# The first microseconds of an MLP kernel: PSUM copies and casts given to ScalarE, and four differences made in halves

## The chip, the cores and the metric

The kernel runs on one core of one Trainium2 chip. The time is that of one execution on the device, in microseconds (us); lower is better. A time here is the median of several executions, and the range is given where it matters.

The engines are called as the profile calls them: PE is TensorE (PEld its weight loads), DVE is VectorE, ACT is ScalarE, POOL is GpSimd, and SP is SyncE, which issues most DMA transfers. PSUM is the memory that the matmuls here write to; SBUF holds the other tiles of the kernel.

## The reference

```python
x:  8 x 1024 x 1024 f32;  w1: 1024 x 4096 f32;  w2: 4096 x 1024 f32
h = x @ w1
h = 0.5 * h * (1 + np.tanh(np.sqrt(2 / np.pi) * (h + 0.044715 * h ** 3)))
return (h @ w2).astype(np.float32)
```

## The kernel before

The kernel works in f16 on blocks of 1024 tokens. Each of the two matrix products is cut into 2 x 2 blocks and done with seven block products in place of eight. For that it needs differences of blocks of x and sums or differences of blocks of the weights; VectorE makes them. In the table, `A_TERMS` gives for each product the two blocks of x that are subtracted, and `B_TERMS` the blocks of weights.

```python
B_TERMS = {1: ("11", SUB, "22"), 2: ("11", None, None), 3: ("12", ADD, "22"), 4: ("21", ADD, "11"),
           5: ("22", None, None), 6: ("11", ADD, "12"), 7: ("21", ADD, "22")}
A_TERMS = {1: ("11", "22"), 2: ("21", "22"), 3: ("11", None), 4: ("22", None),
           5: ("12", "11"), 6: ("21", "11"), 7: ("12", "22")}
```

Products 3 and 4 use a block of x as it is; products 2 and 5 use a block of the weights as it is. For each chunk of 128 columns of a half of w1 the source has the products in the order 4, 5, 1, 2, 3, 7, 6, with 4 matmuls each; product 6 of a chunk stands behind product 5 of the next.

The first 1024 tokens are brought in by the core itself. Eight tiles of 128 tokens are loaded as f32, transposed on TensorE into PSUM, and copied from PSUM to SBUF as f16. The copies are shared by two engines:

```python
def x_first():
    ...
    for a in (1, 0):                       # tokens 512..1023 first, then 0..511
        for q in range(NQ):                # NQ = 4 tiles of 128 tokens
            load_in_order(flat(xn), x2[r0:r0 + P, :])
            for k in (1, 0):
                ps = psum()
                ...                        # 4 transposes by matmul with the identity
                eng = nc.vector.tensor_copy if k == 0 else nc.scalar.copy
                eng(out=blocks[f"{a + 1}{k + 1}"][:, :, q * P:(q + 1) * P], in_=...)
        if a:
            xs.make(2)                     # difference for product 2
    return xs
```

The weights of the first product come in quads of four chunks. The first quad is loaded column by column, so that work can start after one column. Each column is two loads, one for each half of w1, and each load is cast to f16 in two pieces:

```python
def load_cols(self, c, n):                 # n columns of 128, from column c
    ...
    for b in range(2):                     # the two halves of w1
        cast = (nc.scalar.copy, pool_copy)[b]
        for k in range(2 * KH - kn, -1, -kn):
            load_in_order(st, w1v[b, :, k:k + kn, cs])
            for a in range(k // KH, (k + kn) // KH):
                cast(out=self.raw[f"{a + 1}{b + 1}"][:, :, cs], in_=...)
```

After that the differences of x and the sums of the first columns are made in the order of the products:

```python
if sb == 0:
    quads.append(MadeQuad(0, True, False))
    xs.make(5)
    cs = quads[0].load_cols(0, 1)
    quads[0].sum(4, cs)
    for m in (1, 3, 7, 6):
        if m != 3:
            xs.make(m)
        quads[0].sum(m, cs)
    for c, n in ((1, 1), (2, 2)):
        cs = quads[0].load_cols(c, n)
        for m in SUMS:
            quads[0].sum(m, cs)
```

The instructions of an engine run in one order, which a scheduler fixes when the kernel is built; it need not be the order of the source.

## Time and profile before

| | before |
|---|---|
| median of 3 executions (range) | 1582.91 us (1581.23 to 1582.93) |
| span of the profiled execution | 1577.2 us |
| TensorE busy | 98% of the span |
| first matmul of the first product | 17.69 us |
| start of the second product | 122.34 us |

These are the lines of part 1 of the profile page of the kernel before: busy time of each engine, share of the span and number of instructions.

```profile
PE 1547.1 (98%) x7808; PEld 767.1 (49%) x7808; DVE 1028.8 (65%) x1291; ACT 467.9 (30%) x784; POOL 202.8 (13%) x290
```

TensorE is the limit, and only what lets it start earlier or pause less can help. The next view is the timeline of TensorE in the kernel before, with start and length in us; then engine, line, operation, names, shapes and count, and in brackets the idle time before the group and who ended it.

```profile
17.69 1.04 PE L285 MATMUL ps<-u 128*128 128x512 f16 x4 [2.45 <-DVE u L112]
19.85 8.82 PE L285 MATMUL ps<-u 128*128 128x512 f16 x27 [1.12 <-POOL u L123]
29.37 4.26 PE L285 MATMUL ps<-u 128*128 128x512 f16 x19 [0.70 <-DVE tmp L112]
34.11 2.32 PE L285 MATMUL ps<-u 128*128 128x512 f16 x10 [0.48 <-DVE tmp L112]
...
119.25 1.02 PE L285 MATMUL ps<-u 128*128 128x512 f16 x4 [0.17 <-DVE tmp L112]
120.44 2.06 PE L285 MATMUL ps<-u 128*128 128x512 f16 x8 [0.17 <-DVE tmp L112]
```

Product 4 of the first chunk starts at 17.69 us. Its four matmuls end, and product 5 waits 1.12 us for GpSimd's casts. Two pauses behind VectorE and one behind ScalarE (0.41 us, at 36.84) follow.

Who works in these stretches is told by the timeline of the other engines in the kernel before (VectorE, ScalarE, GpSimd):

```profile
15.28 0.69 DVE L250 CAST u<-ps 128x512 f16<-128x512 f32 x1 [0.64 <-PE ps L241]
16.07 2.70 DVE L112 TENSOR_TENSOR u<-u 128x2048 f16<-128x2048 f16 x3
15.87 1.14 ACT L185 CAST u<-gc 128x512 f16<-128x512 f32 x2 [0.44 <-DMA gc<-in_w_dram]
33.72 1.04 ACT L147 CAST u<-gc 128x1024 f16<-128x1024 f32 x1 [4.37 <-DMA gc<-in_w_dram]
17.71 2.08 POOL L123 CAST u<-gc 128x512 f16<-128x512 f32 x2 [16.41 <-DMA gc<-in_w_dram]
```

VectorE copies the last block until 15.97 us and then goes straight into differences of x. GpSimd needs 2.08 us for two casts, where ScalarE needs 1.14 us for two of the same size. ScalarE stands idle for 4.37 us in front of a cast of the next quad (L147), because its column hasn't landed.

The chain of waits of the kernel before, followed back from the matmuls at 45 us, has these pieces among others (start, length, what):

```profile
17.71 2.09 POOL u L123 x2
...
27.68 6.01 DMA gc<-in_w_dram
...
33.72 1.04 ACT u L147
34.77 2.03 ACT g L295 x4
```

### The profile page before, as it was taken

What the parts mean: (1) busy time and instruction counts of PE and PEld (TensorE: products, weight loads), DVE (VectorE), ACT (ScalarE), POOL (GpSimd) and SP (SyncE); (2) the same over time, 40 slices, a digit from 0 to 9 for tenths busy, and PEclk for the clock granted to TensorE, in tenths of its full rate; (3) what the DMA queues carried; (4) which work ended last, traced back from release to release, by engine and by line L of the source; (5) the groups of instructions that cost most, each with busy time, mean ns of one, the idle gap of its engine ahead of it and who ended that gap; (6) DMA issues with size and microseconds to landing.
All of it is one profiled execution on the core that took longest, in us unless ns stands there. A gap on an engine that the chain in (4) does not pass through costs nothing.

```text
span 1577.2 us, 20360 instructions
## 1 busy us (share of the span) xinstructions
PE 1547.1 (98%) x7808; PEld 767.1 (49%) x7808; DVE 1028.8 (65%) x1291; ACT 467.9 (30%) x784; POOL 202.8 (13%) x290
## 2 busy tenths in 40 slices
PE   7999999999899999999999999999999999999998
PEld 4444444444344455444554445544554445544454
DVE  6875967678775567555665647656575556655564
ACT  4645024410144111441124410344004430044210
POOL 2241010033310012000120001200121001200000
PEclk9999999999999999999999999999999999999999
DMA  9999852399965567735696446954569445663164
GB/s 303 340 327 340 246 205 97 122 302 327 399 184 144 200 252 271 233 107 191 247 314 200 157 153 246 358 151 179 179 239 355 135 186 192 243 234 134 54 233 167
DMA packets 165634, 352.64 MB, mean 224 GB/s; under 512 B 72736, under 2 KB 78880, under 8 KB 164640
## 3 DMA queue, kind: packets, MB, share of 16 engines
q1 hardware_dynamic: 146944, 278.97, 51.1%
q0 software_dynamic: 18592, 72.37, 13.9%
q8 instruction: 61, 1.00, 0.3%
q14 instruction: 37, 0.30, 0.1%
HBM read 272.63 MB, written 93.32 MB: 232 GB/s over the span
## 4 chain that ended last, share of the span: by engine, by line
PE 86%; DMA 8%; DVE 3%; issue 1%; ACT 1%; POOL 0%; SPq 0%; DVEq 0%; ACTq 0%; POOLq 0%
PE ps L285 47%; PE ps L567 33%; PE ps L523 6%; DMA u<-w_d 2%; DVE u L112 2%; DMA u<-raw_d 2%; DMA gc<-in_w_dram 1%; DVE tmp L112 1%; DMA out_dram<-tmp 1%; DMA in_d<-u 1%; DVE gc L112 1%; DMA w_d<-u 1%; DMA xb<-in_x_dram 0%; DMA u<-in_x_dram 0%; DMA u<-in_d 0%
## 5 line engine op out<-in xcount | busy, mean ns | idle before, releaser
L285 PE MATMUL ps<-u 128*128 128x512 f16 x3584 | 782.1, 380 | 10.5 <-ACT tmp L349 4.5
L112 DVE TENSOR_TENSOR tmp<-tmp,ps 128x512 f32<-128x512 f32 x580 | 395.8, 685 | 301.4 <-ACT tmp L349 113.7
L285 PEld LDWEIGHTS <-u 128*128 128x128 f16 x3584 | 351.5, 98 | 438.6 <-issue 17.2
L567 PE MATMUL ps<-u,gc 128*128 128x512 f16 x1792 | 389.7, 379 | 3.9 <-DVE gc L112 3.6
L567 PEld LDWEIGHTS <-gc 128*128 128x128 f16 x1792 | 175.2, 98 | 216.0 <-DVE gc L112 4.6
L295 ACT ACTIVATE g<-tmp 128x512 f16<-128x512 f32 x256 | 161.0, 630 | 287.4 <-DVE tmp L112 287.4
L567 PE MATMUL ps<-u,g 128*128 128x512 f16 x1024 | 223.6, 379 | 0.0
L112 DVE TENSOR_TENSOR u<-u 128x2048 f16<-128x2048 f16 (+2 forms) x170 | 183.4, 1112 | 20.9 <-DMA u<-raw_d 12.3
L295 ACT ACTIVATE g<-ps 128x512 f16<-128x512 f32 x256 | 151.8, 596 | 98.4 <-PE ps L285 97.8
L567 PEld LDWEIGHTS <-g 128*128 128x128 f16 x1024 | 100.2, 98 | 119.6
L112 DVE TENSOR_TENSOR gc<-g,g 128x2048 f16<-128x2048 f16 x112 | 132.9, 1220 | 15.8 <-PE ps L567 15.8
L112 DVE TENSOR_TENSOR u<-u,ps 128x512 f32<-128x512 f32 x144 | 95.7, 681 | 68.7 <-ACT tmp L624 37.3
L381 POOL DMA_DIRECT2D out_dram<-tmp x72 | 39.5, 548 | 778.4 <-ACT tmp L617 593.1
L523 PE MATMUL ps<-u,gc 128*128 128x256 f16 x960 | 109.8, 273 | 0.7
L349 ACT COPY tmp<-ps 128x512 f32<-128x512 f32 x128 | 73.0, 570 | 95.5 <-PE ps L285 95.5
L523 PEld LDWEIGHTS <-gc 128*128 128x128 f16 x960 | 93.8, 98 | 12.8 <-issue 1.8
L112 DVE TENSOR_TENSOR gc<-u 128x2048 f16<-128x2048 f16 x60 | 73.2, 1219 | 39.3 <-PE ps L567 39.3
L112 DVE TENSOR_TENSOR tmp<-ps,tmp 128x512 f32<-128x512 f32 x128 | 88.2, 689 | 5.9 <-PE ps L285 1.1
L112 DVE TENSOR_TENSOR u<-tmp,ps 128x512 f32<-128x512 f32 x24 | 16.5, 687 | 74.8 <-PE ps L567 65.1
L112 DVE TENSOR_TENSOR u<-g,g 128x2048 f16<-128x2048 f16 x48 | 59.4, 1277 | 0.0
L617 ACT COPY tmp<-ps 128x512 f32<-128x512 f32 x24 | 14.1, 586 | 152.0 <-PE ps L567 152.0
L624 ACT COPY tmp<-ps 128x512 f32<-128x512 f32 x24 | 14.0, 585 | 133.5 <-PE ps L567 132.8
(32 smaller groups left out, 351.0 us busy)
## 6 DMA issues: line engine op xcount, KB each, us to landing
u<-w_d SPq DMA_DIRECT2D x172, 512.0 KB, 7.8
u<-raw_d SPq DMA_DIRECT2D x136, 512.0 KB, 7.1
u<-in_d SPq DMA_DIRECT2D x84, 512.0 KB, 6.8
gc<-in_w_dram SPq DMA_DIRECT2D x48, 512.0 KB, 6.5
w_d<-u POOLq DMA_DIRECT2D x40, 512.0 KB, 7.3
out_dram<-tmp POOLq DMA_DIRECT2D x72, 256.0 KB, 3.8
raw_d<-u SPq DMA_DIRECT2D x32, 512.0 KB, 10.0
xb<-in_x_dram POOLq DMA_DIRECT2D x56, 256.0 KB, 11.0
```

The lines of the kernel that those rows point to most:

```text
L112: nc.vector.tensor_tensor(out=out, in0=in0, in1=in1, op=op)
L285: nc.tensor.matmul(bank, lhsT=ops[m][:, k, cs], rhs=xs[m][:, k, :], start=(first and k == 0), stop=(k == KH - 1), skip_group_check=not first,)
L295: gelu_last[0] = nc.scalar.activation(out=g[b][:, c, :], in_=src, func=GELU)
L349: nc.scalar.copy(out=v, in_=pb)
L381: return queue.dma_start(out=out2[r0:r0 + P, o0:o0 + OH], in_=src)
L523: nc.tensor.matmul(bank[:, i * HO:(i + 1) * HO], lhsT=t[:, c, i * P:(i + 1) * P], rhs=y[j][:, c, :], start=(first and i == 0 and c == 0), ...
L567: nc.tensor.matmul(banks[q], lhsT=a, rhs=pieces[c // QC][:, c % QC, :], start=(first and c == 0), stop=(c == NI - 1), skip_group_check=not ...
L617: nc.scalar.copy(out=c21, in_=ps)
L624: nc.scalar.copy(out=c12, in_=ps)
```

## The change

The intent is to shorten the way to the first products. Three things change. (1) The second half of the first column is cast by ScalarE and no longer by GpSimd. (2) The four differences 5, 1, 7 and 6 are made in two halves of 256 tokens: the first halves as soon as two of the last four token tiles have been copied, the second halves where the whole ones stood. (3) All the PSUM copies of the first tokens go to ScalarE, which takes eight of them from VectorE.

```diff
-                cast = (nc.scalar.copy, pool_copy)[b]
+                cast = pool_copy if b and c else nc.scalar.copy
...
-        def make(self, *ms):
+        def make(self, *ms, cols=slice(None)):
             for m in ms:
                 u, v = A_TERMS[m]
-                self[m] = unit(KH, HT)
-                tt(self[m], self.blocks[u], self.blocks[v], SUB)
+                if m not in self:
+                    self[m] = unit(KH, HT)
+                tt(self[m][:, :, cols], self.blocks[u][:, :, cols], self.blocks[v][:, :, cols], SUB)
...
-                    eng = nc.vector.tensor_copy if k == 0 else nc.scalar.copy
-                    eng(
+                    nc.scalar.copy(
                         out=blocks[f"{a + 1}{k + 1}"][:, :, q * P:(q + 1) * P],
                         in_=ps.rearrange("p (j t) -> p j t", t=P),
                     )
+                if a == 0 and q == 1:
+                    xs.make(5, 1, 7, 6, cols=slice(0, HT // 2))
...
-            xs.make(5)
+            rest = slice(HT // 2, HT)
+            xs.make(5, cols=rest)
...
-                    xs.make(m)
+                    xs.make(m, cols=rest)
```

## The prediction

> **What bounds the kernel now.** TensorE. The page has PE busy 98% of 1577.2 us, and the idle time before its matmul groups adds up to only about 22 us. The change touches the start alone: by the instruction order of the two built kernels, PE, ACT, DVE and POOL work the same list of jobs after the first blocks, and the DMA queue's order does not change at all. So all that can be won lies before 37 us, after which PE runs 27 us without a pause (timeline).
>
> **What the start costs now** (timeline, waits, granted clock):
> - x tiles land about 1.29 us apart until 14.04 us; transposes end at 15.24.
> - First real matmuls at 17.69 us, released by DVE: the first w1 column lands at 15.85, ACT casts it until 17.01, but DVE is in a 1.22 us difference (m=5) until 17.29 and only then makes the sum.
> - PE then waits 1.12 us for POOL, whose two casts of the second column take 2.08 us (ACT: 1.14 us).
> - Pauses of 0.70, 0.48 and 0.41 us follow at 29.4, 34.1, 36.8, behind DVE (busy nearly without a break from 20 to 36 us) and behind ACT, which sits 4.37 us in front of a cast whose column has not landed, with gelus queued behind.
> - The granted clock is 0.5 from 18.77 to 25.60 us, about 2.9 us lost from 19.85 on. That is twice the 3.413 us window of the Trainium skill ("TensorE: Matmul & The Clock Gate", The HAM clock gate), so the trace agrees; its phase runs freely.
>
> **What the change moves.**
> - Eight PSUM copies of 0.69 us go from DVE to ACT (0.585 us): ACT then does two per x tile, 1.19 us in 1.29 us. It just keeps up.
> - Four differences (1.22 us each) become eight halves, estimated at 0.65 us; four of them run before the last tokens. About 2.6 us of DVE work leaves the crowded stretch after 16 us.
> - The second column's casts take 1.14 us on ACT instead of 2.08 on POOL: product 5 can start at about 18.9 instead of 19.85.
> - Against it: the last PSUM copy stands on ACT between the two casts of the first column, so it waits for the landing at 15.85; the second halves of 5 and 1 and the first sum then end at about 18.7. I expect the FIRST matmul about 1 us LATER (18.7 us), then no pause before product 5.
> - The cast of the third load comes before a gelu on ACT, so the first load of the next quad is issued about 3 us earlier (now 26.74), and ACT's 4.37 us stall mostly goes.
>
> **Sum.** Pauses of 2.7 us fall to about 1; 1 us is lost at the first matmul; the half clock ends one window earlier or at the same time (0 to 1.7 us). Net gain 0.5 to 2.5 us, expected 1.4 us. Later waits (3.02 us at 173.9, 4.52 at 431) hang on loads that PE's progress releases, so I expect the gain to be kept.
>
> **Time:** 1581.3 us, 8 in 10 between 1579.0 and 1583.2; the three runs of before spread over 1.7 us. Faster by over 2%: 0.01; within 2%: 0.98; slower: 0.01.
>
> **What would show it.** First matmul after 17.69; gap before product 5 near zero; DVE's m=5, 1, 7, 6 halves starting near 12 us; ACT's first 128x1024 cast of the next quad with little wait; PE continuous, about 1 to 2 us ahead at 40 us.
>
> **What would make it wrong.** ACT falling behind the transposes; the clock gate's phase, at the start or at the 4.52 us wait, hiding or doubling the gain; the DMA-filled stretch 137 to 166 us giving the gain back at 173.9.

## The result, and the profile after

| | before | after |
|---|---|---|
| median of 4 executions (range) | 1582.92 us (1581.23 to 1583.69) | 1579.90 us (1578.62 to 1584.12) |
| ratio, 95% interval | | 0.9987 (0.9967 to 1.0007) |
| span of the profiled execution | 1577.2 us | 1576.9 us |
| first matmul of the first product | 17.69 us | 18.59 us |
| start of the second product | 122.34 us | 118.95 us |

A ratio is the mean time of one kernel's fast runs over that of the other's of the same rounds, so it isn't quite the ratio of the medians that are quoted. The kernel after was run again later in five executions beside eleven of the kernel before, with medians of 1576.61 and 1582.44 us and a ratio of 0.9972 (0.9947 to 0.9998). So there is a small gain, some 0.1 to 0.3%, which a single set of rounds could hardly tell from nothing.

The same views of the kernel after. First part 1 of its page:

```profile
PE 1547.7 (98%) x7808; PEld 768.5 (49%) x7808; DVE 1022.3 (65%) x1287; ACT 474.7 (30%) x794; POOL 197.6 (13%) x288
```

VectorE has lost 6.5 us of work and ScalarE has gained 6.8; TensorE is as busy as it was. Its timeline:

```profile
18.59 14.23 PE L287 MATMUL ps<-u 128*128 128x512 f16 x53 [3.44 <-DVE u L112]
33.70 85.41 PE L287 MATMUL ps<-u 128*128 128x512 f16 x395 [0.88 <-DVE tmp L112]
118.95 4.26 PE L570 MATMUL ps<-u,g 128*128 128x512 f16 x19
```

TensorE starts 0.90 us later, but then pauses just once before the second product, for 0.88 us at 33.70. The pause before product 5 is gone, and so are all the small pauses to the end. The second product starts 3.39 us earlier.

The timeline of the other engines in the kernel after (VectorE, ScalarE, GpSimd):

```profile
13.60 3.10 DVE L112 TENSOR_TENSOR u<-u 128x1024 f16<-128x1024 f16 x5 [0.73 <-ACT u L250]
16.91 4.08 DVE L112 TENSOR_TENSOR u<-u 128x1024 f16<-128x1024 f16 x9 [0.21 <-ACT u L250]
15.77 0.62 ACT L185 CAST u<-gc 128x512 f16<-128x512 f32 x1 [0.44 <-DMA gc<-in_w_dram]
16.30 0.58 ACT L250 CAST u<-ps 128x512 f16<-128x512 f32 x1
16.77 0.62 ACT L185 CAST u<-gc 128x512 f16<-128x512 f32 x1
32.27 1.04 ACT L147 CAST u<-gc 128x1024 f16<-128x1024 f32 x1
21.21 1.17 POOL L123 CAST u<-gc 128x512 f16<-128x512 f32 x2 [19.90 <-DMA gc<-in_w_dram]
```

The last copy from PSUM (L250) stands on ScalarE between the two casts of the first column, so it waits for that column to land. This is why the first matmul comes later. The first halves of the differences run before 16.7 us, in time that VectorE had spent on copies or had been waiting. ScalarE no longer waits in front of the next quad's cast (L147). GpSimd's first pair of casts is now that of a later column and takes 1.17 us.

The busy time of the engines from 20 to 34 us (columns: stretch, its length; busy time and instructions of PE, PEld, DVE, ACT, POOL; granted clock; DMA share; GB/s), for the kernel before:

```profile
20.00:34.00 14.00, 12.93 (x46) 5.04 (x45) 12.93 (x22) 4.94 (x9) 4.87 (x5) 0.80 0.90 285
```

And for the kernel after:

```profile
20.00:34.00 14.00, 13.12 (x53) 5.47 (x52) 11.08 (x20) 8.21 (x14) 5.34 (x6) 0.86 0.97 332
```

VectorE is busy for 11.08 us there in place of 12.93, and TensorE fits in 53 matmuls for 46 (a few records can be missing); its granted clock is also higher in this stretch, 0.86 for 0.80. Busy time is work done, and not work that waits: it is one sign only, and below it doesn't tell the better kernels from the others.

**An account of the start.** From the starts of single matmuls in the trace one can say where the time up to the second product goes. The matmuls need 0.216 us each at full clock, some 96.7 us in all; the rest is the start of the first matmul, the pauses, and the time lost at half clock. A pause is counted here from start to start, so a pause that the timeline shows as x costs about x + 0.16 us. The parts add up to the last column within 0.2 us.

| kernel | first matmul | pauses before 40 us | lost at half clock | pauses after 40 us | second product starts |
|---|---|---|---|---|---|
| before | 17.69 | 3.66 | 2.53 | 1.78 | 122.34 |
| after | 18.59 | 1.16 | 2.50 | 0 | 118.95 |
| after, second time | 18.40 | 1.21 | 2.50 | 0 | 118.89 |

The gain of 3.39 us is thus −0.90 for the later start, +2.50 for pauses at the start, +0.03 for the clock and +1.78 for pauses after 40 us.

**Where the lead goes.** In the first pair of traces the lead of 3.39 us ended as 0.3 us. After 122 us both kernels have the same waits: near 170 us, near 430 us and near 1516 us. These vary from execution to execution of the same kernel, and so do the windows of half clock that may follow them. The profile of the kernel after has such windows at 17.1 to 23.9, 170.7 to 174.1 and 426.7 to 433.5 us; that of before at 18.8 to 25.6 and 431.8 to 435.2 us only. In the second trace of the kernel after, those at 16.8 and 170.4 us were the only ones, and its span was 1573.2 us. The four to eleven executions of one kernel in the same rounds spread over 2.5 to 23 us. This is why the start of the second product is used below to compare kernels: it stands ahead of all those waits. In the two traces of the kernel after it repeated to 0.06 us; but the last kernel of this document, whose instructions come in the same order until 163 us, has it at 119.34 us (first matmul 18.86). So one program's mark varies by some 0.45 us in three traces, and a smaller difference between kernels says nothing. The whole time is given too.

### The profile page after: what moved, and what is told of

Read it like the earlier page. It is cut to its first block, busy times and chain, and to the rows that moved or that the text cites. A ratio compares the mean times of both kernels' runs of the same rounds, so it can differ in the third digit from the quotient of the medians.

```text
span 1576.9 us, 20366 instructions
## 1 busy us (share of the span) xinstructions
PE 1547.7 (98%) x7808; PEld 768.5 (49%) x7808; DVE 1022.3 (65%) x1287; ACT 474.7 (30%) x794; POOL 197.6 (13%) x288
## 4 chain that ended last, share of the span: by engine, by line
PE 89%; DMA 6%; DVE 3%; issue 1%; SPq 0%; ACT 0%; DVEq 0%; ACTq 0%
PE ps L287 48%; PE ps L570 35%; PE ps L526 6%; DMA raw_d<-u 2%; DVE u L112 2%; DMA u<-raw_d 2%; DMA u<-w_d 1%; DVE tmp L112 1%; DMA gc<-in_w_dram 1%; DVE gc L112 1%; SPq L120 0%; DMA u<-in_d 0%; ACT tmp L352 0%; ACT u L185 0%; DVE tmp L446 0%
## 5 line engine op out<-in xcount | busy, mean ns | idle before, releaser
L112 DVE TENSOR_TENSOR u<-tmp,ps 128x512 f32<-128x512 f32 x24 | 16.5, 688 | 74.8 <-PE ps L570 65.1
```

Of the source, the lines that this page charges most:

```text
L112: nc.vector.tensor_tensor(out=out, in0=in0, in1=in1, op=op)
```

## The experiments

### The three parts, one at a time and two at a time

The theory at this point: either one of the three parts carries the gain alone, or they need each other. The rival to all three was that ScalarE's stall of 4.37 us, which the chain of waits shows, is what was removed, by whichever part.

**Part 1 alone: the casts.**

```diff
-                cast = (nc.scalar.copy, pool_copy)[b]
+                cast = pool_copy if b and c else nc.scalar.copy
```

> Before, with only the casts of the first columns all on ScalarE. Work-moved theory (each part helps by the work it takes off the crowded engine): first real matmul stays at 17.7 us, the 1.12 us pause before product 5 falls under 0.3, and the first matmul of the second product (before: 122.34 us, after: 118.95) comes 0.8 to 1.5 us earlier. Order theory (the gain is that the halved differences make the build place ScalarE's first cast of the next quad behind four gelus): the pause before product 5 goes, but ScalarE still stands about 4 us before that cast, the pauses near 34 and 37 us stay, and the second product starts at most 0.7 us earlier.

Measured: 1582.08 us beside 1581.00, ratio 1.0013 (0.9977 to 1.0049). First matmul 17.92, second product 122.22 us. The pause before product 5 is gone, but the pauses before 40 us still add up to 3.45 us: what was saved at 19 us is waited for at 24.0 and 33.5.

**Part 3 alone: the copies.**

```diff
-                    eng = nc.vector.tensor_copy if k == 0 else nc.scalar.copy
-                    eng(
+                    nc.scalar.copy(
```

> Before, with only all PSUM copies of the first x blocks on ScalarE. Both theories: ScalarE keeps up with the transposes, first matmul at 17.7 us (the whole difference of 1.22 us still stands before the first sum), pause before product 5 stays near 1.1 us, second product starts within 0.5 us of before's 122.34. Work-moved theory allows up to 0.5 us gain, order theory none.

Measured: 1582.83 us, ratio 1.0014 (0.9991 to 1.0038). First matmul 17.70, second product 123.17 us. There's no gain; the pauses only move, 3.23 us before 40 us and 3.02 after.

**Part 2 alone: the halves.** The edit is that of `make`, of the early `xs.make(5, 1, 7, 6, cols=slice(0, HT // 2))` and of `rest`, as in the change.

> Before, with only the differences in halves; copies stay shared by VectorE and ScalarE, casts as before. Both: first matmul near 17.4 us, since only one half stands before the first sum, and a pause of about 1.5 us before product 5 (POOL casts). Order theory: ScalarE's wait before its first cast of the next quad falls under 1 us, the pauses near 29, 34 and 37 us shrink to under 1 us together, and the second product starts 2.0 to 3.4 us earlier than before's 122.34. Work-moved theory: about 1 us earlier.

Measured: 1578.39 us, ratio 0.9994 (0.9969 to 1.0020). Second product 119.57 us: 2.77 of the 3.39 us are here. Of my two theories the one called order theory had forecast 2.0 to 3.4 us and the one called work-moved theory about 1 us, so the size is nearer to the first; a test of ScalarE's cast, on which that theory hung, speaks against it below. But the first matmul comes at 19.89 us, where an early start had been expected. The timelines of TensorE and VectorE of this kernel show it:

```profile
19.89 13.76 PE L288 MATMUL ps<-u 128*128 128x512 f16 x54 [4.83 <-DVE u L112]
...
14.24 2.50 DVE L112 TENSOR_TENSOR u<-u 128x1024 f16<-128x1024 f16 x4
16.66 0.68 DVE L251 CAST u<-ps 128x512 f16<-128x512 f32 x1
17.26 0.68 DVE L112 TENSOR_TENSOR u<-u 128x1024 f16<-128x1024 f16 x1
17.86 0.68 DVE L251 CAST u<-ps 128x512 f16<-128x512 f32 x1
```

VectorE makes four early halves in one go, 2.50 us, in front of its own copies of the last tiles. The last copy ends at 18.54 us, where it ended at 15.97 before.

**Parts 1 and 2: after, with the copies shared again.**

```diff
-                    nc.scalar.copy(
+                    eng = nc.vector.tensor_copy if k == 0 else nc.scalar.copy
+                    eng(
```

> After, with the PSUM copies shared by VectorE and ScalarE as before. If the copies on ScalarE cost the late first matmul, it comes near 17.4 us instead of 18.59, with under 0.6 us of pause before product 5, and the second product starts 0.5 to 1.2 us before after's 118.95. If the copies are needed for the gain (VectorE too full to make the halves early), it starts no earlier than 118.95.

Measured: 1580.55 us, ratio 1.0013 (0.9973 to 1.0053). First matmul 19.75 us, again late behind VectorE's own copies; pauses of 0.67 us before 40 us and 1.92 after; second product 120.98 us. I had expected a first matmul at 17.4 us here too, for the same wrong reason: I had left out that halves moved ahead also stand in front of the copies on the engine that makes both.

**Parts 2 and 3: after, with the casts as before.**

```diff
-                cast = pool_copy if b and c else nc.scalar.copy
+                cast = (nc.scalar.copy, pool_copy)[b]
```

> After, with the casts of the first columns split over ScalarE and GpSimd as before. First matmul near 18.6 us as in after; GpSimd's casts end near 19.6 us while product 4 at half clock lasts until about 20.3 us, so no pause before product 5 of over 0.3 us, and the second product starts within 0.5 us of 118.95: then the casts give nothing by themselves. If the casts are needed, product 5 waits 0.8 us or more and the second product comes that much later.

Measured: 1576.83 us beside 1581.99, ratio 0.9937 (0.9866 to 1.0007). First matmul 18.83, second product 119.31 us, against 118.95 with all three parts. That difference is no larger than one program's mark varies, so the casts aren't told from nothing.

What follows: the halves carry the gain. The copies on ScalarE are what lets the halves go early without holding up the copies themselves: first matmul 18.59 with them, 19.75 without. At the second product they gain 2.03 us where the casts are on ScalarE (120.98 to 118.95), but 0.26 us where they are not (119.57 to 119.31), so their worth isn't settled. The casts alone win nothing.

### Does ScalarE's stall before the next quad cause the pauses?

Rival theory: in the kernel before, ScalarE waits 4.37 us for a column of the next quad, with gelus queued behind; TensorE then waits for banks of PSUM. The experiment takes the waiting cast off ScalarE in the kernel before:

```diff
-                        nc.scalar.copy if k else pool_copy,
+                        nc.scalar.copy if k and self.q != 1 else pool_copy,
```

> Before, with the next quad's casts (the 128x1024 ones of the second quad) all on GpSimd, so ScalarE has nothing that waits for a landing among its gelus between 29 and 40 us; the differences stay whole, VectorE's order in the first 40 us stays that of before. Order theory (ScalarE standing in front of a cast makes the pauses near 34 and 37 us): these two pauses and ScalarE's 4.4 us wait go, first matmul and the pause of 1.1 us before product 5 stay, second product starts about 1.2 us or more before 122.34. Crowded-VectorE theory (the whole differences after 16 us make the pauses): the pauses stay within 0.4 us of before's, second product within 0.6 us of 122.34.

Measured: 1580.57 us, ratio 0.9968 (0.9909 to 1.0027). Second product 122.31 us, as before. The timelines of TensorE and ScalarE of this kernel:

```profile
33.25 5.12 PE L285 MATMUL ps<-u 128*128 128x512 f16 x23 [0.94 <-DVE tmp L112]
...
28.12 0.58 ACT L349 COPY tmp<-ps 128x512 f32<-128x512 f32 x1
32.63 0.63 ACT L295 ACTIVATE g<-tmp 128x512 f16<-128x512 f32 x1 [3.93 <-DVE tmp L112]
```

ScalarE still stands idle from 28.7 to 32.6 us, but now it waits for VectorE. Behind the wait for the DMA that the kernel before shows, a wait for VectorE had been hidden; it is only 0.44 us shorter. This theory falls, as far as it is about ScalarE's cast. VectorE kept the order of before until 40 us here, so whether another order of VectorE and TensorE matters isn't tested by it.

### Is it the crowd on VectorE?

Second theory: between 18 and 36 us VectorE is behind with its work, and what the halves do is to take half of four differences out of that stretch. If so, making the late halves whole again, with nothing else changed in the source, should bring the pauses back. The result is still right: the first 256 tokens are simply computed twice.

```diff
-            rest = slice(HT // 2, HT)
+            rest = slice(0, HT)
```

> After, with the second halves of the four differences made over the full width (1.22 us instead of 0.65 us each; correct, the early halves are simply overwritten), so VectorE has about 2.3 us more to do after the last token block. Crowded-VectorE theory (the halves gain because half of this work is gone before the crowded stretch): the sum of TensorE's pauses before 40 us and after grows by about 2 us and the second product starts at 121 to 122.5 us, close to the kernels without halves (122.2 to 123.2). If the halves gain only by another arrangement of the start, it stays within 0.8 us of after's 118.95.

Measured: 1585.14 us (1580.30 to 1598.02) beside 1582.44, ratio 1.0033 (0.9991 to 1.0075). The timeline of TensorE:

```profile
18.72 3.63 PE L287 MATMUL ps<-u 128*128 128x512 f16 x16 [3.38 <-DVE u L112]
22.66 2.28 PE L287 MATMUL ps<-u 128*128 128x512 f16 x9 [0.32 <-DVE u L112]
25.75 5.77 PE L287 MATMUL ps<-u 128*128 128x512 f16 x26 [0.81 <-DVE tmp L112]
33.54 4.65 PE L287 MATMUL ps<-u 128*128 128x512 f16 x13 [2.02 <-DVE tmp L112]
...
122.38 1.89 PE L570 MATMUL ps<-u,g 128*128 128x512 f16 x8
```

The pauses are back, 3.91 us before 40 us and 1.40 after, and the second product starts at 122.38 us, as this theory had forecast. But it isn't shown that VectorE's work alone does it, for three reasons.

- The build gave another order here as well. VectorE's and ScalarE's lists each differ from those of after in more than ten places. TensorE takes product 3 of the first chunk behind products 4 and 5 of the second, as in before, where after takes it ahead of them. The loss, 3.43 us, is also larger than the 2.3 us of work that I had estimated to be put back.
- Another order can cost nearly as much. The kernels with 32 and with 20 transposes below have the same edit otherwise, as many instructions on VectorE, ScalarE and GpSimd, and a full clock, but another order: 121.36 against 119.05 us.
- VectorE's busy time from 20 to 34 us doesn't go with the result: 11.83 us here, but 13.02 with the halves alone and 12.96 with the last copy on VectorE, which keep the lead, and 12.93 in before.

What is shown is the edit that counts: the eight kernels with late halves start the second product at 118.9 to 121.4 us, the five with whole late differences at 122.2 to 123.2 us. Whether the halves gain by less work after 16 us or by the order that the build then chooses stays open; a run with late whole differences in the order of after would tell.

### Is a start before 18.6 us worth anything?

The change pays 0.90 us at the first matmul. Giving the very last copy back to VectorE should buy most of it back:

```diff
-                    nc.scalar.copy(
+                    last = a == 0 and q == NQ - 1 and k == 0
+                    (nc.vector.tensor_copy if last else nc.scalar.copy)(
```

> After, with only the very last PSUM copy (fourth token block, first half of the columns) back on VectorE, so that it does not stand on ScalarE behind a cast that waits for a landing. First real matmul 17.3 to 17.6 us instead of 18.59, product 5 near 18.8, pauses after it as in after (about 1.2 us in all), second product 0.3 to 1.1 us before 118.95. If the late first matmul of after has another cause, it stays near 18.6.

Measured: 1576.67 us beside 1581.99, ratio 0.9947 (0.9887 to 1.0006). First matmul at 18.00 us, 0.6 earlier (I had expected 17.3 to 17.6). But the pause before 33.60 us grows from 0.88 to 2.09 us, 1.03 us less is lost at half clock, and the second product starts at 118.90 us, within 0.05 us of after. What is gained at the front is waited for, mostly at 33.6. The build's order differs from that of after here too.

### Does the half clock at the start cost anything?

After the last transpose TensorE is idle for some 3.4 us. In that time, at 17.10 us, the granted clock falls to 0.5, and it stays there until 23.93 us, for 6.83 us, twice the window of 3413 ns that the Trainium skill gives ("TensorE: Matmul & The Clock Gate", Part 1: The HAM clock gate); matmuls then follow each other every 0.427 us in place of 0.216, as that page has it too. My prediction counted this as up to 1.7 us to be won. The experiment keeps TensorE busy with transposes of the identity while it would be idle:

```diff
                 xs.make(2)
+        fill = psum()
+        for i in range(32):
+            nc.tensor.matmul(fill[:, :P], lhsT=identity, rhs=identity,
+                             is_transpose=True, start=True, stop=True)
         return xs
```

> After, with 32 transposes of the identity into a spare PSUM bank behind the last transpose, to keep TensorE busy until the first real matmul; they write nothing that is used. Clock theory (the half clock from 17 to 24 us comes of the idle 3.4 us and costs 2.5 us on twelve matmuls): the granted clock stays at 1.0, no matmul of the first ones is 0.43 us apart, the fill ends by 18.6 us, and the second product starts 1.5 to 2.6 us before 118.95, less what VectorE then makes TensorE wait. If transposes do not count as activity for the clock gate, the half clock stays and nothing is won.

Measured: 1581.06 us, ratio 0.9966 (0.9906 to 1.0025). Nothing is lost at half clock any more, but pauses grow to 4.96 us before 40 us, and the second product starts at 121.36 us. This run doesn't settle the question, for the build put the other engines' instructions in another order; it shows instead what an order is worth, with the next run beside it.

With 20 in place of 32 the order of every engine is exactly that of after, the 20 transposes apart:

> After, with 20 transposes of the identity into a spare PSUM bank behind the last transpose; with this number the built order of all engines is exactly that of after, unlike the 32 of w1_fill. Clock theory: the fill runs from 15.2 to about 17.4 us, the granted clock stays 1.0 over the first matmuls, twelve matmuls lose no 0.21 us each, and the second product starts 1.5 to 2.6 us before 118.95. Landing theory (what follows 25 us waits for w1 columns that land at 25.6 and 27.0 us and for VectorE behind them, so a faster TensorE only waits longer): the half clock goes, but the pauses between 24 and 35 us grow from 1.2 to 2.5 us or more, and the second product starts at most 0.8 us earlier.

Measured: 1578.40 us (one run of six at 1594.27), ratio 0.9992 (0.9957 to 1.0027). Here are the windows of 16 to 20 and 20 to 24 us (columns as above; the granted clock is the third number from the end), of after:

```profile
16.00:20.00 4.00, 1.41 (x4) 0.59 (x5) 3.79 (x9) 3.14 (x7) 0.00 (x0) 0.64 1.20 291
20.00:24.00 4.00, 4.00 (x11) 1.37 (x10) 2.60 (x8) 2.15 (x4) 1.17 (x2) 0.51 1.10 344
```

The same of the kernel with 20 transposes:

```profile
16.00:20.00 4.00, 2.73 (x17) 1.51 (x16) 3.56 (x8) 3.15 (x7) 0.00 (x0) 1.00 1.19 292
20.00:24.00 4.00, 3.04 (x15) 1.27 (x13) 3.15 (x8) 2.37 (x5) 1.17 (x2) 1.00 1.10 348
```

The clock is full, and from 20 to 24 us TensorE is idle for a quarter of the time instead. Its timeline:

```profile
18.12 4.92 PE L292 MATMUL ps<-u 128*128 128x512 f16 x22 [1.27 <-DVE u L112]
24.01 6.85 PE L292 MATMUL ps<-u 128*128 128x512 f16 x31 [0.97 <-DVE tmp L112]
32.93 5.34 PE L292 MATMUL ps<-u 128*128 128x512 f16 x24 [2.07 <-DVE tmp L112]
...
119.05 5.13 PE L575 MATMUL ps<-u,g 128*128 128x512 f16 x23
```

Nothing lost at half clock, 0.47 us earlier at the first matmul, and yet the second product starts at 119.05 us, 0.10 us later than after. Pauses of 3.36 + 0.88 us have taken the place of 1.16 us of pauses and 2.50 us of half clock. The half clock at the start lies off the critical path: faster matmuls only arrive sooner at waits. Most of it is waited for at 24.0 and 32.9 us, behind VectorE. TensorE still goes on 0.77 us ahead of after there (32.93 for 33.70), and loses that in four short pauses between 45 and 81 us, whose cause wasn't looked into.

### The kernel after once more

The kernel after itself, in the same rounds as the kernels with whole late halves and with 20 transposes:

> The changed kernel itself once more, for the size of the effect and for how well the trace repeats: first matmul within 0.3 us of 18.59, one pause near 33.7 us, second product within 0.4 us of 118.95; total 1 to 4 us under before of the same rounds, with single runs spread over 5 us or more through the waits near 170, 430 and 1516 us and the half clock after them.

Measured: 1576.61 us (1575.00 to 1579.62), beside 1582.44 (1576.64 to 1589.86), ratio 0.9972 (0.9947 to 0.9998). First matmul 18.40, second product 118.89 us: the start repeats to 0.2 us in these two traces, the rest of the execution doesn't.

### A version that beats both

All the kernels so far wait 2.75 to 4.0 us near 170 us, in the second product of the first token block. The timelines of TensorE and VectorE of the kernel after there:

```profile
170.46 14.81 PE L570 MATMUL ps<-u,gc 128*128 128x512 f16 x60 [3.00 <-DVE gc L112]
...
163.44 4.63 DVE L112 TENSOR_TENSOR u<-u 128x2048 f16<-128x2048 f16 x4
...
169.18 4.63 DVE L112 TENSOR_TENSOR gc<-g,g 128x2048 f16<-128x2048 f16 x4
```

VectorE makes four sums of w2 that only product 7 needs (4.63 us), in front of the differences that product 1 needs now. The edit moves the call behind product 1:

```diff
             tt(d[q], u[q], d[q], SUB)
-        add(7, over="21")
         blocks = x_transpose(xb, load_in_order)
         for q, ps in product2(g, 1, pieces(1), rb, True):
             tt(d[q], d[q], ps, ADD)
+        add(7, over="21")
```

> After, with one thing moved that all traces point to: in the second product of the first two token blocks the four sums of w2 for product 7 are made behind product 1 instead of in front of it, so they (4.6 us of VectorE) no longer stand before the differences of gelu outputs that product 1 waits for. Expected: first matmul, the one pause at 33.7 us and the start of the second product (118.9) as in after; the 3.0 to 3.5 us pause near 170 us under 0.5 us, and no half clock right after it (1.7 us more); total 3 to 5 us under after's, about 1572 to 1575 us, 7 to 10 us under before of the same rounds. If the pause hangs on something behind VectorE (a store that lands at 163 us, gelu banks), it only moves and the total stays within 1.5 us of after's.

Measured: 1571.98 us (1570.13 to 1576.76, six runs) beside 1581.69 (eleven runs), ratio 0.9946 (0.9927 to 0.9964). This is the only kernel besides the second look at after whose interval leaves out 1, and it does so clearly. It is 0.5%. It beats before in the same rounds; that it beats after is told only across rounds (1571.98 against 1576.61 and 1579.90 us). The timelines of TensorE and VectorE, from 159.7 us:

```profile
159.70 26.50 PE L570 MATMUL ps<-u,gc 128*128 128x512 f16 x122
...
164.11 1.22 DVE L112 TENSOR_TENSOR gc<-g,g 128x2048 f16<-128x2048 f16 x1
```

TensorE runs through; the first difference for product 1 is made at 164.11 us in place of 169.18. And as there is no pause, no window of half clock follows it in this trace. The start wasn't quite as expected: first matmul 18.86 us, a pause of 1.76 us from start to start at 33.75, and the second product 0.39 us later than in after, with the same order of instructions.

## Why the prediction was right, and where not

The time was right: 1581.3 us were predicted, 1579.0 to 1583.2 as the range, and 1579.90 us were measured. In the later rounds the kernel after had 1576.61 us, below the range, beside a kernel before of 1582.44 us; with a spread of this size the first median was partly luck. By the ratios the gain is some 2 us in the first rounds and 4.4 us in the later ones, where 1.6 us had been predicted.

- **"I expect the FIRST matmul about 1 us LATER (18.7 us), then no pause before product 5."** Right: 18.59 us, and no pause. The reason fits the timeline: the last copy stands on ScalarE behind the cast that waits for the landing (15.77 to 17.4 us). Giving that copy back to VectorE brought 0.59 of the 0.90 us back (18.00 us).
- **"It just keeps up."** Right: a copy from PSUM took 0.585 us on ScalarE and 0.69 on VectorE, and the transposes ended at 15.15 us for 15.24.
- **"Pauses of 2.7 us fall to about 1."** Right: 0.88 us of idle time are left before 40 us. Counted from start to start it is 3.66 to 1.16 us, so the saving was 2.50 where I had counted about 1.7.
- **"ACT's 4.37 us stall mostly goes."** It did go, and the next quad's first load was issued at 23.75 us for 26.74. But the weight that I gave it was wrong: without the stall, in the kernel with the next quad's casts on GpSimd, the pauses before 40 us still add up to 3.18 us (3.66 before), and the second product starts as late.
- **"All that can be won lies before 37 us, after which PE runs 27 us without a pause."** This step failed, and so did its ground, that "the change touches the start alone": the lists of jobs are the same, but the build put them in another order on TensorE, VectorE and ScalarE, and not at the start alone. I had looked at the 27 us behind 37 and not at the rest. Small pauses at 63.9, 65.1, 71.5, 89.8, 119.2, 120.4 and 121.5 us, 1.78 us in all, are gone after the change. More than half of the gain at the second product (3.39 us) is what I had not counted: the start itself gives 1.63 us (2.50 + 0.03 − 0.90), and the later pauses give 1.78. That the 1.63 is near the 1.4 us predicted is partly luck: 1.7 for the pauses less 1 for the first matmul leaves some 0.7 us that I had put on the clock, which gave 0.03, and the pauses gave 0.8 more than I had counted. Why the later pauses go isn't settled. At 115.40 us in the kernel before, VectorE makes two whole sums of w2 in a row (3.19 us) ahead of a chunk's additions; in the kernel after they stand singly between the additions (1.22 us each). So it is another order from the build, at a place that the change doesn't touch; the kernel with shared copies keeps 1.92 us of such pauses although it has the halves.
- **"The half clock ends one window earlier or at the same time (0 to 1.7 us)."** It ended at 23.93 us for 25.60, but TensorE also began later, and the time lost is the same (2.50 us for 2.53), so the 0 was right. But as a thing to be won it was wrong in kind: with the clock at full from the start, nothing is won.
- **"About 2.6 us of DVE work leaves the crowded stretch after 16 us."** This was in the text as one point of several, and it names the edit that carries the gain. From 20 to 34 us VectorE is busy for 1.85 us less (12.93 to 11.08), and making the late halves whole takes the whole lead away. But that run changed the order too, and other kernels with halves are as busy as before there (13.02 and 12.96 us) and still keep the lead. So the point that less work is how the halves gain is argued and not shown.
- **"I expect the gain to be kept."** Half right: at 170 us the lead was still 3.41 us. After that the waits of either kernel vary by more than the lead, and in the first pair of traces only 0.3 us were left.

That GpSimd's two casts took 2.08 us before and 1.17 us after agrees with what the Trainium skill says of the shared port ("SBUF — State Buffer", SBUF: two separate sides: the read and write port pair that VectorE and GpSimd share is held for a whole instruction, and the loser waits; it counts an operation of VectorE with two SBUF inputs, against a GpSimd operation that reads SBUF). In the kernel before, VectorE was in a subtraction of two SBUF tensors for most of the first cast, which took 1.52 us, and the second took 0.61 us with VectorE idle. No run here separates the two engines on purpose, so the lock is argued and not shown. It made no difference to the whole: taking those casts off GpSimd alone won nothing.

The halves themselves are what the skill recommends for such a place ("Perfetto Trace Analysis", Optimizing Scalar/DVE Operations): "If Scalar/Vector aren't saturated, but are causing bubbles on other engines, breaking up instructions may allow work to be completed sooner." VectorE is busy for 65% of the span and, in the kernel before, for 92% from 20 to 34 us (12.93 of 14). The trace agrees in so far as four first halves were made by 16.7 us; why TensorE pauses less afterwards is the open point above.

## What to carry to other kernels

Look for work of an engine that could run before the crowded stretch, and split it so that a part of it can; but see what that part then stands in front of on the same engine (here its own PSUM copies, 2.5 us, until those went to ScalarE). A wait that the chain of waits names may hide a second one of nearly the same length behind it, so take it away alone before you believe in it. A small edit can change the order of every engine in the built program: compare the built orders before you put a gain down to the work that you moved. Compare small changes at a mark ahead of the waits that vary, and look along the whole stage for small pauses, not just at the first ones.

## What the Trainium skill lacked or had wrong

- "TensorE: Matmul & The Clock Gate", Part 4: PE-mode transpose, says that the full clock doesn't engage for transposes. Here it did, with f32 transposes (the page's times there are for bf16): in the kernel before the first record of a full clock came at 8.53 us, when TensorE had done nothing else, and their spacing fell from 213 to 109 ns. In the kernels with 20 and 32 more transposes the clock was also 1.00 from 16 to 24 us, where after had 0.64 and 0.51; but the kernel with whole late halves had 1.00 there without them, so this second point is no proof.
- The same page, Part 1: The HAM clock gate, puts the price of the start at half clock below 1% of a typical kernel's span, and 2.50 of 1577 us agrees. It doesn't say that even this may lie off the critical path: here the 2.50 us at half clock were taken away with every engine's order unchanged, and the second product started 0.10 us later, not earlier.
- "Perfetto Trace Analysis", Identifying Performance Opportunities, tells how to find what blocks an engine, but I found no page that says that a wait shown in the trace can hide another one behind it: ScalarE's 4.37 us for a DMA became 3.93 us for VectorE when the first was taken away.
- "Perfetto Trace Analysis", Optimizing Scalar/DVE Operations, recommends breaking up instructions, but I found no page that warns that a part moved ahead delays what the same engine has to do next: four early halves (2.50 us) moved VectorE's last copy from 15.97 to 18.54 us and the first matmul to 19.89 us.
- I found no page that gives a figure for the spread of a whole kernel's time from execution to execution: here it was 2.5 to 23 us of some 1580, and the traces show waits near 170, 430 and 1516 us, and windows of half clock behind them, that differ from execution to execution.
